# Entry of the first MLP product in a decoder layer: GpSimd's steps on VectorE, tile pairs, a norm factor read from PSUM, ten plain column tiles for six

## The chip, the cores and the metric

The kernel runs on one NeuronCore of a Trainium2 chip. TensorE (PE) multiplies into PSUM; VectorE (DVE), ScalarE (ACT) and GpSimd (POOL) do the elementwise work; SyncE (SP) and ScalarE issue transfers. Each engine runs its own queue in order and waits on semaphores. The metric is the device time of one execution in microseconds, the median of several runs.

## What is computed

One layer of a decoder trunk over 512 tokens and a width of 2048, in float32: a mixer (a recurrence and sparse attention), an MLP, and a gated addition of a per-layer embedding (PLE). Cut to the part in question:

```python
y = jnp.concatenate([rms_norm(y_lru, gnorm_lru[i]), rms_norm(y_nsa, gnorm_nsa[i])], axis=-1)
h = h + rms_norm(y @ w_out[i], norm_mix_post[i])
f = jnp.square(jax.nn.relu(rms_norm(h, norm_mlp_pre[i]) @ mlp_w1[i])) @ mlp_w2[i]
h = h + rms_norm(f, norm_mlp_post[i])
h = h + jax.nn.sigmoid(h @ ple_gate[i]) * (p[i] @ ple_proj[i])
```

`mlp_w1` is 2048 x 8192, so its product has 64 column tiles of 128.

## The kernel before

**Layout.** Activations lie transposed: 128 channels on the partitions, 512 tokens in the free dimension, so the stream of width 2048 is 16 rows of 128x512. They lie in eight tiles `y`, each a pair of rows (`y_row(k)` is one row). A float32 product is made of three matmuls (`mm3`): weights and activations are split into a high part in the TensorE format, by ScalarE, and the rest, by VectorE, and hi x hi, hi x lo and lo x hi are summed in PSUM.

**Strips.** TensorE's program is a list of strips. A strip is 128x512 of a weight matrix, four blocks of 128 (k = 0 to 3), 12 matmuls. `go` runs over the strips: at strip j it fires the hooks due at j, splits the weights of strip j + 4 (`shi` by ScalarE, `slo` by VectorE, rings of five), lets up to two finished PSUM results be evicted, and issues the matmuls of strip j, with the hooks due at its quarters in between. `at(j, fn)` hangs a function on a strip's quarter. Every engine's queue is in the order in which `go` issues; a table of constants at the top of the file says when.

**Two forms of product.** `add_plain` multiplies a few column tiles at once, four strips each, with 512 columns per matmul. Its first strips are interleaved over the tiles, so that each activation row is used by all tiles as it comes. `pair_a` takes two column tiles at once in seven half products (Winograd's form of Strassen's), 14 strips with 256 columns per matmul; it needs seven sets of activation units (`ua`), made from sums of quarters of `y` (`combo_sum`, `prep_g`, `prep_a`), and sums of weights (`sums`).

**The entry of the first MLP product** (`back`). `b0` is the first strip of five of the PLE product (`add_ple`), `bk` the first strip behind them. While those run, the mixer's norm factor is made: `rms_a` multiplies the squares' sum with ones on TensorE and takes the root on VectorE and ScalarE, `rms_b` spreads it over the partitions by eight small matmuls into a PSUM bank and copies it to `rb` (`Ro`). Then come, for each row k, `h1_a` (times `Ro`; even k on VectorE, odd k on GpSimd), `h1_b` (times the gain `norm_mix_post`, plus `x`; and ScalarE makes the high part of the unit `up[k]`, times `norm_mlp_pre`), `h1_c` (the low part; ScalarE squares the row), `h1_d` (GpSimd adds the square to `msum`), and later `h1_e` (the row times `norm_mlp_pre`). Tiles 0 to 3 and then 4 and 5 of the product are plain and are evicted once the MLP's factor `Rm` is there. From `Rm` on, `y_scale` multiplies halves of `y` by it, on VectorE and on GpSimd, and the seven sets of units are made; then 29 pairs follow.

**Transfers.** Weights come through five buffers of 512 KB (`raw`), loaded by SP, which also loads `x` and stores PLE results. The gate product at the end has the same form: plain tiles, then pairs; its norm's scaling (L1588) and two of its `combo_sum` steps are on GpSimd as well.

Of the kernel before, what the change touches and what calls it, by code (L numbers as in the profile page):

```python
# [37 lines left out]
SL = 0.7  # L38
RMT = 11.5
WO = (-12, -11, -10, -9, -7, -5)  # L40
NPL = 6
# [21 lines left out]
PMX = (14.75, 16.5, 18.5, 20.5, 22.5, 24.5, 26.5)  # L63
# [10 lines left out]
RO0 = 1.75  # L74
RO1 = 0.5
HO = 2.75
# [3 lines left out]
PMG = (13.5, 15, 18, 20)  # L80
PLE1 = 5
# [54 lines left out]
class Build:  # L136
# [138 lines left out]
    def add_col(self, src, units, evict, lead=FW, extra=()):  # L275
        q, st, extra = {}, [], list(extra)
        b, n, step = len(self.strips), src.shape[-1] // 512, 2 if extra else 1

        def load(h):
            q[h] = self.raw_tile()  # L280
            self.nc.sync.dma_start(q[h], src[:, h * 1024:(h + 1) * 1024])

        def mm(s):
            def f(j, k):
                if s + k == 0:
                    st.append(self.bank())
# [153 lines left out]
    def y_scale(self, e, a, b, i, rb):  # L440
        t = self.y[4 * a + i][:, :, b * H:(b + 1) * H]
        e.tensor_tensor(t, t, rb[:, b * H:(b + 1) * H].unsqueeze(1).to_broadcast([P, 2, H]), op=ALU.mult)  # L442

    def prep_g(self, p):
        for i in range(4):
            if p in (1, 2):
                self.y_scale(self.nc.gpsimd, p - 1, 1, i, self.T["R"])
            else:
                self.combo_sum(1 if p == 6 else 3, (self.y[i], self.y[4 + i]), None)

    def prep_a(self, ua, p, inside=False, scale=True, lo=None):
        v, g = self.nc.vector, self.nc.gpsimd
        rb = self.T["R"]
# [46 lines left out]
    def rms_b(self, name):  # L500
# [15 lines left out]
    def run(self):  # L516
# [10 lines left out]
        self.rings = {}  # L527
        dp = self.pool("dram", space=bass.MemoryType.DRAM)
# [448 lines left out]
    def mid(self):  # L977
# [66 lines left out]
        def y_out(m):  # L1044
            def f(ps):
# [4 lines left out]
                if m >= KT - 2:  # L1050
# [337 lines left out]
    def back(self):  # L1388
# [23 lines left out]
        def load_x(k):  # L1412
            t = x_tile() if k % 8 < 4 else self.z_tile("xz")
            nc.sync.dma_start(t, A["xT"][:, k:k + 2, :])
            T["xt", k], T["xt", k + 1] = t[:, 0], t[:, 1]

        def h1_a(k):
            (g if k % 2 else v).tensor_tensor(xs(k), xs(k), T["Ro"], op=ALU.mult)

        def h1_b(k):  # L1420
            y = xs(k)
            v.scalar_tensor_tensor(y, y, V[:, V_MIXPOST + k:V_MIXPOST + k + 1], T["xt", k], op0=ALU.mult, op1=ALU.add)  # L1422
            act.activation(up[k][:, 0], y, AF.Copy, scale=V[:, V_MLPPRE + k:V_MLPPRE + k + 1])
            self.store(self.h1_d[k], y)

        def h1_c(k):
            y = xs(k)
            v.scalar_tensor_tensor(up[k][:, 1], y, V[:, V_MLPPRE + k:V_MLPPRE + k + 1], f32(up[k][:, 0]),  # L1428
                                   op0=ALU.mult, op1=ALU.subtract)
            act.activation(self.msum if k == 0 else T["xt", k], y, AF.Square)  # L1430

        def h1_d(k):
            xt = T["xt", k]
            if k == KT - 1:
                sq_last.append(xt)
            elif k:
                g.tensor_tensor(self.msum, self.msum, xt, op=ALU.add)
# [3 lines left out]

        def h1_at(k):
            return b0 + max(HO, SL * (k - 3) + HO)

        def plain_a(m0):
            def f(i, ps, st):
# [3 lines left out]
                v.tensor_tensor(t, ps, T["Rm"], op=ALU.mult)  # L1450
                v.scalar_tensor_tensor(t, t, 0.0, t, op0=ALU.max, op1=ALU.mult)
# [21 lines left out]
        for k in range(0, 8, 2):  # L1473
            at(b0 - 3 if k < 4 else b0 + 2, load_x, k)
# [3 lines left out]
        if NPL > 4:  # L1478
            self.add_plain(bk + 16, [A["mlp_w1"][m] for m in range(4, NPL)], up, plain_a(4), "Rm", (-7, -6))
        for k in range(KT):  # L1480
            if k >= 8 and k % 2 == 0:
                at(h1_at(k - 7) + 3.75, load_x, k)
            at(max(h1_at(k) + GE, b0 + GE0), h1_e, k)
            for i, fn in enumerate((h1_a, h1_b, h1_c, h1_d)):
                at(h1_at(k) + i, fn, k)
        at(bk + RMT, self.sqrt_table)
        at(bk + RMT, lambda: self.rms_a([self.msum] + sq_last, D, "m"))
# [10 lines left out]
        at(bk + 28.5, open_fb)  # L1498
# [174 lines left out]
        for p, j in zip(ORDER, GX):  # L1673
            at(bg + j, self.prep_a, ue, p, True, False, g if p in GS else None)
# [97 lines left out]
```

## Time and profile before

| What | Value |
|---|---|
| Median of 3 runs | 2459.36 us (2458.16 to 2459.91) |
| Profiled execution, its own time | 2458.5 us |
| Its span, first to last instruction | 2456.7 us, 34978 instructions |
| TensorE matmuls | 2342.9 us busy, 95% of the span |
| VectorE | 1544.3 us, 63% |
| ScalarE | 1076.8 us, 44% |
| GpSimd | 243.5 us, 10% |
| Mean granted TensorE clock | 0.979 of full speed |

Matmuls are pipelined and their ends are modelled, so a busy TensorE is not TensorE at its peak: a matmul of 512 columns is shown with 0.39 us at full clock while the next starts 0.227 us after it. Steps are therefore read from one start to the next. Some matmul records are missing.

### The profile page before, as it was taken

What the parts mean: (1) busy time and instruction counts of PE and PEld (TensorE: products, weight loads), DVE (VectorE), ACT (ScalarE), POOL (GpSimd) and SP (SyncE); (2) the same over time, 40 slices, a digit from 0 to 9 for tenths busy, and PEclk for the clock granted to TensorE, in tenths of its full rate; (3) what the DMA queues carried; (4) which work ended last, traced back from release to release, by engine and by line L of the source; (5) the groups of instructions that cost most, each with busy time, mean ns of one, the idle gap of its engine ahead of it and who ended that gap; (6) DMA issues with size and microseconds to landing.
All of it is one profiled execution on the core that took longest, in us unless ns stands there. A gap on an engine that the chain in (4) does not pass through costs nothing.

```text
span 2456.7 us, 34978 instructions
## 1 busy us (share of the span) xinstructions
PE 2342.9 (95%) x13178; PEld 2046.3 (83%) x13178; DVE 1544.3 (63%) x2543; ACT 1076.8 (44%) x2008; POOL 243.5 (10%) x238
## 2 busy tenths in 40 slices
PE   7999999989999778999999998999999999997899
PEld 6788888777788658999999997888888888886688
DVE  6364755588746789888888886333333333335898
ACT  5354655478733445444444444333223223223454
POOL 4000000134400440000000000000000000112420
PEclk9999999999999889999999999999999999998999
DMA  5452232422234532343433333434333333233644
GB/s 191 159 180 93 99 108 97 133 89 84 82 129 164 191 103 98 127 138 130 136 131 134 134 135 126 159 116 133 112 112 137 121 103 131 101 112 128 223 142 138
DMA packets 114093, 316.75 MB, mean 129 GB/s; under 512 B 11298, under 2 KB 16674, under 8 KB 113924
## 3 DMA queue, kind: packets, MB, share of 16 engines
q1 hardware_dynamic: 94708, 275.13, 34.0%
q10 hardware_dynamic: 19216, 39.39, 4.2%
q8 instruction: 103, 1.69, 0.3%
q14 instruction: 66, 0.54, 0.1%
HBM read 270.37 MB, written 44.11 MB: 128 GB/s over the span
## 4 chain that ended last, share of the span: by engine, by line
PE 62%; DVE 6%; issue 2%; DMA 1%; ACT 1%; POOL 0%; ACTq 0%; DVEq 0%; SPq 0%; POOLq 0%
PE ps_mm L165 20%; PE ps_mm L163 20%; PE ps_mm L164 20%; DVE slo L156 1%; DVE cx L156 1%; DMA fk<-f_d 1%; DVE y L1592 1%; PE ps_t L487 0%; DVE y L442 0%; POOL pz L1619 0%; ACT shi L155 0%; DVE y L1422 0%; DVE cy L156 0%; DVE y L1588 0%; DMA pz<-pp_d 0%
## 5 line engine op out<-in xcount | busy, mean ns | idle before, releaser
L156 DVE TENSOR_TENSOR slo<-raw,shi 128x512 fp32r<-128x512 f32 x802 | 580.0, 729 | 743.1 <-ACT shi L155 727.4
L155 ACT ACTIVATE shi<-raw 128x512 fp32r<-128x512 f32 x804 | 502.2, 629 | 870.5 <-PE ps_mm L164 748.4
L163 PE MATMUL ps_mm<-cx,shi 128*128 128x512 f32 (+1 forms) x2044 | 707.7, 346 | 25.4 <-ACT shi L155 19.8
L164 PE MATMUL ps_mm<-cx,shi 128*128 128x512 f32 (+1 forms) x2044 | 702.1, 343 | 15.0 <-DVE cx L1428 7.5
L165 PE MATMUL ps_mm<-cx,slo 128*128 128x512 f32 (+1 forms) x2044 | 704.0, 344 | 13.0 <-DVE slo L156 10.7
L165 PE MATMUL ps_mm<-cy,slo 128*128 128x512 f32 (+1 forms) x1604 | 555.0, 346 | 6.4 <-DVE slo L156 6.4
L163 PE MATMUL ps_mm<-cy,shi 128*128 128x512 f32 (+1 forms) x1604 | 555.4, 346 | 3.7 <-ACT shi L155 2.0
L164 PE MATMUL ps_mm<-cy,shi 128*128 128x512 f32 (+1 forms) x1604 | 554.9, 346 | 4.1 <-DVE cy L1428 4.1
L163 PEld LDWEIGHTS ps_mm<-cx,shi 128*128 128x128 f32 x2044 | 393.0, 192 | 70.8 <-ACT shi L155 23.5
L165 PEld LDWEIGHTS ps_mm<-cx,slo 128*128 128x128 f32 x2044 | 392.5, 192 | 62.7 <-DVE slo L156 16.6
L164 PEld LDWEIGHTS ps_mm<-cx,shi 128*128 128x128 f32 x2044 | 393.3, 192 | 57.8 <-DVE cx L1428 8.8
L165 PEld LDWEIGHTS ps_mm<-cy,slo 128*128 128x128 f32 x1604 | 305.8, 191 | 44.6 <-DVE slo L156 8.0
L163 PEld LDWEIGHTS ps_mm<-cy,shi 128*128 128x128 f32 x1604 | 305.9, 191 | 40.8 <-ACT shi L155 2.6
L164 PEld LDWEIGHTS ps_mm<-cy,shi 128*128 128x128 f32 x1604 | 305.9, 191 | 40.5 <-DVE cy L1428 4.8
L155 ACT ACTIVATE shi<-wsum 128x512 fp32r<-128x512 f32 x204 | 126.5, 628 | 163.9 <-PE ps_mm L164 87.8
L156 DVE TENSOR_TENSOR slo<-wsum,shi 128x512 fp32r<-128x512 f32 x204 | 138.7, 687 | 44.8 <-ACT shi L155 44.8
L1530 POOL TENSOR_TENSOR msum<-msum,fsq 128x512 f32<-128x512 f32 x13 | 16.9, 1297 | 1288.7 <-ACT fsq L1526 1288.7
L1257 POOL TENSOR_SCALAR al_P<-al_P,ar_sts 128x512 f32<-128x512 f32 (+3 forms) x128 | 74.2, 601 | 63.8 <-ACT al_ph L1279 29.3
L163 PE MATMUL ps_mm<-y,shi 128*128 128x256 f32 x272 | 76.4, 281 | 1.2 <-ACT shi L155 1.2
L1247 ACT ACTIVATE al_P<-al_P,ar_stm 128x512 f32<-128x512 f32 (+3 forms) x128 | 70.4, 554 | 16.1 <-DVE ar_stm L1242 15.8
L165 PE MATMUL ps_mm<-y,slo 128*128 128x256 f32 x272 | 76.1, 280 | 0.8 <-DVE slo L156 0.8
L164 PE MATMUL ps_mm<-y,shi 128*128 128x256 f32 x272 | 75.9, 279 | 0.0
(356 smaller groups left out, 2336.3 us busy)
## 6 DMA issues: line engine op xcount, KB each, us to landing
raw<-in_mlp_w_dram SPq DMA_DIRECT2D x254, 512.0 KB, 3.7
raw<-in_w_in_dram SPq DMA_DIRECT2D x64, 512.0 KB, 3.5
raw<-in_w_out_dram SPq DMA_DIRECT2D x32, 512.0 KB, 3.5
fk<-f_d SPq DMA_DIRECT2D x32, 512.0 KB, 5.0
raw<-in_ple_gate_dram SPq DMA_DIRECT2D x32, 512.0 KB, 4.8
f_d<-z ACTq DMA_DIRECT2D x29, 512.0 KB, 2.8
y<-in_xT_dram SPq DMA_DIRECT2D x16, 256.0 KB, 6.2
raw<-in_w_v_dram SPq DMA_DIRECT2D x8, 512.0 KB, 4.3
```

Source lines behind the costliest of these rows:

```text
L155: nc.scalar.activation(hi, src, AF.Copy)
L156: (eng or nc.vector).tensor_tensor(lo, src, f32(hi), op=ALU.subtract)
L163: mm(ps, whi, ahi, start=start, stop=False)
L164: mm(ps, whi, alo, start=False, stop=False)
L165: mm(ps, wlo, ahi, start=False, stop=stop)
L1247: act.activation(PP[qt, b], PP[qt, b], AF.Exp, scale=-1.0, bias=st["mn"][:, qt, b:b + 1], accum_out=st["sm"][:, qt, b:b + 1])
L1257: pool.tensor_scalar(PP[qt, b], PP[qt, b], st["sm"][:, qt, b:b + 1], 1.0, op0=ALU.mult, op1=ALU.mult)
L1530: g.tensor_tensor(self.msum, self.msum, sq, op=ALU.add)
L1592: v.scalar_tensor_tensor(y, y, V[:, V_MLPPOST + k:V_MLPPOST + k + 1], T["h"][k], op0=ALU.mult, op1=ALU.add)
```

## The change

The scalings, sums and squares of the entry that were on GpSimd go to VectorE, and most steps take a pair of rows (1024 columns) instead of one. `norm_mix_post` is multiplied in by ScalarE when a row of the `w_out` product is evicted, so `h1_b`'s operation with a gain becomes a plain add, and the sum of squares runs in a tile of two rows, `hs`. `rms_b("o")` makes no copy: the scalings read the PSUM bank. The evicted plain tiles are squared by ScalarE. Four more column tiles are plain: four interleaved, two one by one (`add_col`), four interleaved; 27 pairs follow. One PLE strip moves to the gate product (`PLE1`). `combo_sum`'s two GpSimd cases go to VectorE in both products. The constants that place the hooks are new.

```diff
-RMT = 11.5
-WO = (-12, -11, -10, -9, -7, -5)
-NPL = 6
+HT = (1.75, 2.75, 4, 4.25, 4.75, 8.5, 10.75, 12.25)
+HB = (0, 0.5, 0.75, 1, 2)
+RMT = 12.5
+WO = (-12, -7.75, -6.75, -5.75)
+NPL = 10
...
-PMX = (14.75, 16.5, 18.5, 20.5, 22.5, 24.5, 26.5)
+PMX = (18.5, 23, 28.25, 32.25, 36.25, 40.25, 38.25)
+YS = (15.25, 0.75)
...
-RO0 = 1.75
-RO1 = 0.5
+RO0 = 0.75
+RO1 = 0.75
...
-PLE1 = 5
+PLE1 = 4
...
         if i == 1:
-            nc.gpsimd.tensor_tensor(y11, y12, y11, op=ALU.subtract)
+            nc.vector.tensor_tensor(y11, y12, y11, op=ALU.subtract)
...
-            nc.gpsimd.tensor_tensor(y12, y22, y12, op=ALU.subtract)
+            nc.vector.tensor_tensor(y12, y22, y12, op=ALU.subtract)
...
+    def y_scale(self, i):
+        t = self.y[i]
+        self.nc.vector.tensor_tensor(t, t, self.T["R"].unsqueeze(1).to_broadcast([P, 2, S]), op=ALU.mult)
...
+        if name in self.direct:
+            self.T["R"] = self.T["R" + name] = ps2
+            return
...
                 act.activation(self.msum if m == 0 else l, y, AF.Square)
-                if m >= KT - 2:
+                act.activation(y, y, AF.Copy, scale=self.vec[:, V_MIXPOST + m:V_MIXPOST + m + 1])
+                if m == KT - 1:
...
+        def h1_a(i):
+            y, x, r = self.y[i], T["xt", i], T["Ro"]
...
+                v.tensor_tensor(y, y, r.unsqueeze(1).to_broadcast([P, 2, S]), op=ALU.mult)
+                v.tensor_tensor(y, y, x, op=ALU.add)
+                h1_hi(2 * i)
+                h1_hi(2 * i + 1)
...
+        def h1_add(i):
+            if i:
+                v.tensor_tensor(T["hs"], T["hs"], T["xt", i], op=ALU.add)
...
-                v.tensor_tensor(t, ps, T["Rm"], op=ALU.mult)
-                v.scalar_tensor_tensor(t, t, 0.0, t, op0=ALU.max, op1=ALU.mult)
+                v.scalar_tensor_tensor(t, ps, 0.0, T["Rm"], op0=ALU.max, op1=ALU.mult)
+                act.activation(t, t, AF.Square)
...
+        for m in range(4, NPL - 4):
+            self.add_col(A["mlp_w1"][m], up, lambda ps, m=m: plain_a(4)(m - 4, ps, one), 8, cond="Rm")
```

How the instructions stand, at two places. VectorE at the first rows behind the mixer's factor (`rbo`, now `ps_t`), before; `y_6710` is the first pair of rows, `y_6711` the second, `cy` and `cx` are units, `slo` is the low part of a weight strip:

```order
L1418 TENSOR_TENSOR y_6710<-y_6710,rbo 128x512
L1418 TENSOR_TENSOR y_6711<-y_6711,rbo 128x512
L156 TENSOR_TENSOR slo<-raw,shi 128x512
L1418 TENSOR_TENSOR y_6712<-y_6712,rbo 128x512
L1422 SCALAR_TENSOR_TENSOR y_6710<-y_6710,vec,xt 128x512 x2
L1422 SCALAR_TENSOR_TENSOR y_6711<-y_6711,vec,xt 128x512 x2
```

VectorE at the same place, now:

```order
L1418 TENSOR_TENSOR y_6710<-y_6710,xt 128x512
L157 TENSOR_TENSOR slo<-raw,shi 128x512
L1431 SCALAR_TENSOR_TENSOR cy<-y_6710,vec,cy 128x512 x2
L1421 TENSOR_TENSOR y_6711<-y_6711,ps_t 128x1024
L1422 TENSOR_TENSOR y_6711<-y_6711,xt 128x1024
L157 TENSOR_TENSOR slo<-raw,shi 128x512
L1431 SCALAR_TENSOR_TENSOR cy<-y_6711,vec,cy 128x512 x2
```

A pair of rows is now finished, units and all, before the next pair is scaled, and a weight split stands between the pair's add and its low parts. ScalarE a little later, at the fourth and fifth pair (`y_6713`, `y_6714`), before; `shi` is the high part of a weight strip, and rows that square `y` write `xt` or `xz`:

```order
L1423 ACTIVATE cx<-y_6713,vec 128x512
L1430 ACTIVATE xz<-y_6713 128x512
L419 DMA h_d<-y_6713 128x512
L155 ACTIVATE shi<-raw 128x512
L1423 ACTIVATE cx<-y_6714,vec 128x512
L1430 ACTIVATE xz<-y_6713 128x512
```

ScalarE at the same place, now:

```order
L1428 ACTIVATE cx<-y_6713,vec 128x512 x2
L1428 ACTIVATE cx<-y_6714,vec 128x512 x2
L1437 ACTIVATE xz<-y_6712 128x1024
L420 DMA h_d<-y_6712 128x2x512
L156 ACTIVATE shi<-raw 128x512
L1437 ACTIVATE xz<-y_6713 128x1024
L420 DMA h_d<-y_6713 128x2x512
```

A weight split there now stands behind the high parts of two whole pairs and the square of a third.

## Rows read from the trace of the kernel before

**Rows 1.** Stretches: us, then busy PE, PEld, DVE, ACT, POOL, PEclk, DMA share, GB/s.

```profile
809.40:871.60 62.20, 44.62 (x168) 33.22 (x166) 49.35 (x50) 32.73 (x56) 32.20 (x22) 0.88 0.49 169
871.60:929.50 57.90, 46.21 (x174) 36.40 (x175) 49.97 (x61) 25.43 (x47) 26.55 (x16) 0.83 0.27 91
929.50:976.80 47.30, 42.76 (x338) 41.91 (x336) 43.86 (x69) 22.68 (x40) 0.00 (x0) 0.96 0.33 112
976.80:996.90 20.10, 20.10 (x170) 20.10 (x169) 17.35 (x28) 8.72 (x15) 0.00 (x0) 1.00 0.39 132
```

**Rows 2.** VectorE's waits, 809 to 872: us in total, times, longest us.

```profile
DVE slo L156 <- ACT shi L155: 9.8, 8, 1.8
```

**Rows 3.** Line 1418, the scaling by the factor: min/median/max ns, first and last start.

```profile
L1418 DVE TENSOR_TENSOR y<-y,rbo x8: 679/1230/1785, 809.4 to 858.6; 128x512 f32<-128x512 f32 x8
L1418 POOL TENSOR_TENSOR y<-y,rbo x8: 1301/1735/1796, 809.4 to 858.1; 128x512 f32<-128x512 f32 x8
```

**Rows 4.** Timeline (start, us, engine, line) of the mixer's norm, ScalarE and TensorE.

```profile
798.54 0.63 ACT L1049 ACTIVATE yl<-y 128x512 f32<-128x512 f32 x1 [3.20 <-DVE y L1048]
...
802.33 0.28 PE L487 MATMUL ps_t<-ones,msum 128*128 128x1 f32 x2
...
804.92 0.48 PE L163 MATMUL ps_mm<-cy,shi 128*128 128x512 f32 x1
...
806.66 2.04 PE L505 MATMUL ps_t<-ident,rsmo 128*128 128x128 f32 x8
...
808.74 0.60 ACT L508 ACTIVATE rbo<-ps_t 128x512 f32<-128x512 f32 x1 [1.74 <-PE ps_t L505]
```

**Rows 5.** Timeline of VectorE, two places where nothing disturbs it.

```profile
816.77 2.06 DVE L1422 SCALAR_TENSOR_TENSOR y<-y,vec,xt 128x512 f32<-128x512 f32 x3
...
2337.22 1.22 DVE L316 TENSOR_TENSOR wsum<-raw 128x1024 f32<-128x1024 f32 x1
2338.35 0.69 DVE L156 TENSOR_TENSOR slo<-raw,shi 128x512 fp32r<-128x512 f32 x1
2338.96 1.22 DVE L320 TENSOR_TENSOR wsum<-wsum,raw 128x1024 f32<-128x1024 f32 x1
```

**Rows 6.** Groups of ScalarE's instructions by line: count, busy us, mean ns, idle before.

```profile
L1423 ACT ACTIVATE cx<-y,vec 128x512 fp32r<-128x512 f32 x10 | 7.2, 724 | 18.1 <-DVE y L1422 17.9
L155 ACT ACTIVATE shi<-raw 128x512 fp32r<-128x512 f32 x11 | 6.8, 619 | 2.7 <-PE ps_mm L164 2.7
...
L1120 ACT ACTIVATE al_kh<-raw 128x1024 fp32r<-128x1024 f32 x4 | 4.2, 1044 | 0.0
```

**Rows 7.** Timeline of TensorE at the MLP's norm.

```profile
871.59 0.58 PE L487 MATMUL ps_t<-ones,msum 128*128 128x1 f32 x2 [2.14 <-POOL msum L1437]
...
875.02 0.77 PE L163 MATMUL ps_mm<-cx,shi 128*128 128x512 f32 x1
...
881.40 1.05 PE L505 MATMUL ps_t<-ident,rsmm 128*128 128x128 f32 x8
882.21 0.47 PE L163 MATMUL ps_mm<-cx,shi 128*128 128x512 f32 x1
```

**Rows 8.** Timeline: a plain strip's weight split; starts of the third and fourth pair.

```profile
1718.22 0.69 DVE L156 TENSOR_TENSOR slo<-raw,shi 128x512 fp32r<-128x512 f32 x1 [2.03 <-ACT shi L155]
...
976.80 0.29 PE L163 MATMUL ps_mm<-cx,shi 128*128 128x256 f32 x1
...
996.91 0.29 PE L163 MATMUL ps_mm<-cx,shi 128*128 128x256 f32 x1
```

**Rows 9.** Line 1047, VectorE on a PSUM source: min/median/max ns, first and last start.

```profile
L1047 DVE TENSOR_TENSOR y<-ps_mm,rbn x16: 680/683/693, 716.6 to 797.1; 128x512 f32<-128x512 f32 x16
```

**Rows 10.** The gate product: one stretch as in rows 1, and GpSimd's groups by line.

```profile
2295.00:2325.00 30.00, 25.50 (x99) 19.91 (x98) 28.59 (x22) 15.00 (x26) 25.16 (x15) 0.90 0.57 197
...
L431 POOL TENSOR_TENSOR y<-y,y 128x512 f32<-128x512 f32 x4 | 6.8, 1741 | 0.0
L427 POOL TENSOR_TENSOR y<-y 128x512 f32<-128x512 f32 x4 | 6.8, 1734 | 38.9 <-DVE cy L156 38.9
```

More of the change, by code (lines that the diff above doesn't have):

```diff
@@ L79 @@
 SF = 0.7
-PMG = (13.5, 15, 18, 20)
-PLE1 = 5
+PMG = (24.25, 24.75)
+PLE1 = 4
 BK = -0.5
@@ L273, in add_plain, with add_col @@
                 self.strips.append(Strip(lambda i=i, s=s: q[i, s // 2][:, (s % 2) * 512:(s % 2 + 1) * 512], mm(i, s)))
-    def add_col(self, src, units, evict, lead=FW, extra=()):
+    def add_col(self, src, units, evict, lead=FW, extra=(), cond="zp"):
         q, st, extra = {}, [], list(extra)
@@ L291, in f @@
                 if s == n - 1 and k == 3:
-                    self.wait.append(("zp", evict, st[0]))
+                    self.wait.append((cond, evict, st[0]))
             return f
@@ L438, in combo_split, with prep_a @@
         self.split(u[:, :, 0, :], u[:, :, 1, :], src, eng=eng)
-    def y_scale(self, e, a, b, i, rb):
-        t = self.y[4 * a + i][:, :, b * H:(b + 1) * H]
-        e.tensor_tensor(t, t, rb[:, b * H:(b + 1) * H].unsqueeze(1).to_broadcast([P, 2, H]), op=ALU.mult)
+    def y_scale(self, i):
+        t = self.y[i]
+        self.nc.vector.tensor_tensor(t, t, self.T["R"].unsqueeze(1).to_broadcast([P, 2, S]), op=ALU.mult)
     def prep_g(self, p):
         for i in range(4):
[L446 to L453, printed above, removed]
+            self.combo_sum(1 if p == 6 else 3, (self.y[i], self.y[4 + i]), None)
+    def prep_a(self, ua, p, inside=False, lo=None):
         Y = [(self.y[i], self.y[4 + i]) for i in range(4)]
-        scale = scale and p in (1, 2)
-        if scale:
-            self.y_scale(v, p - 1, 0, 0, rb)
         if p == ORDER[-1] and inside:
@@ L466, in ready @@
         def ready(i):
-            if scale and i:
-                self.y_scale(v, p - 1, 0, i, rb)
             if p == 6:
@@ L527, in run @@
         self.rings = {}
+        self.direct = ("o",)
         dp = self.pool("dram", space=bass.MemoryType.DRAM)
@@ L1414, in load_x @@
             nc.sync.dma_start(t, A["xT"][:, k:k + 2, :])
[L1415 to L1424, printed above, removed]
@@ L1426, in h1_c @@
-        def h1_c(k):
-            y = xs(k)
-            v.scalar_tensor_tensor(up[k][:, 1], y, V[:, V_MLPPRE + k:V_MLPPRE + k + 1], f32(up[k][:, 0]),
-                                   op0=ALU.mult, op1=ALU.subtract)
[L1430 to L1437, printed above, removed]
+            T["xt", k // 2] = t
@@ new lines, in h1_a @@
+        def h1_a(i):
+            y, x, r = self.y[i], T["xt", i], T["Ro"]
+            if i == 0:
+                for a in range(2):
+                    v.tensor_tensor(y[:, a], y[:, a], r, op=ALU.mult)
+                    v.tensor_tensor(y[:, a], y[:, a], x[:, a], op=ALU.add)
+                    h1_hi(a)
+            else:
+                v.tensor_tensor(y, y, r.unsqueeze(1).to_broadcast([P, 2, S]), op=ALU.mult)
+                v.tensor_tensor(y, y, x, op=ALU.add)
+                h1_hi(2 * i)
+                h1_hi(2 * i + 1)
+            self.store(self.h1_d[2 * i:2 * i + 2].rearrange("a p n -> p a n"), y)
@@ new lines, in h1_hi, with h1_lo, h1_sq @@
+        def h1_hi(k):
+            act.activation(up[k][:, 0], xs(k), AF.Copy, scale=V[:, V_MLPPRE + k:V_MLPPRE + k + 1])
+        def h1_lo(k):
+            v.scalar_tensor_tensor(up[k][:, 1], xs(k), V[:, V_MLPPRE + k:V_MLPPRE + k + 1], f32(up[k][:, 0]),
+                                   op0=ALU.mult, op1=ALU.subtract)
+        def h1_sq(i):
+            if i == 0:
+                T["hs"] = self.sum_tile("hs").rearrange("p (a n) -> p a n", a=2)
+            act.activation(T["xt", i] if i else T["hs"], self.y[i], AF.Square)
@@ L1477, in back @@
         self.add_plain(bk, [A["mlp_w1"][m] for m in range(4)], up, plain_a(0), "Rm", (-8.5, -7.5, -6.5, -5.5))
[L1478 to L1485, printed above, removed]
+        one = {}
+        for m in range(4, NPL - 4):
+            self.add_col(A["mlp_w1"][m], up, lambda ps, m=m: plain_a(4)(m - 4, ps, one), 8, cond="Rm")
+        bl = len(self.strips)
+        self.add_plain(bl, [A["mlp_w1"][m] for m in range(NPL - 4, NPL)], up, plain_a(NPL - 4), "Rm", (-8, -7, -6, -5))
+        for i in range(KT // 2):
+            j = b0 + HT[i]
+            if i >= 4:
+                at(b0 + HT[i - 4] + 2.25, load_x, 2 * i)
+            for o, fn, k in zip(HB, (h1_a, h1_lo, h1_lo, h1_sq, h1_add), (i, 2 * i, 2 * i + 1, i, i)):
+                at(j + o, fn, k)
+            for a in range(2):
+                at(j + GE, h1_e, 2 * i + a)
         at(bk + RMT, self.sqrt_table)
-        at(bk + RMT, lambda: self.rms_a([self.msum] + sq_last, D, "m"))
+        at(bk + RMT, lambda: self.rms_a([T["hs"][:, 0], T["hs"][:, 1]], D, "m"))
+        for i in range(KT // 2):
+            at(bk + YS[0] + YS[1] * i, self.y_scale, i)
         at(bk + RMT + 1.25, self.rms_b, "m")
@@ L1491, in back @@
         for m in range(NPL, DFF // P, 2):
-            self.pair_a(b, A["mlp_w1"], m, ua, sink_a(m), first=m == NPL and NPL == 4, offs=WO if m == NPL and NPL > 4 else None, last=m == DFF // P - 2)
+            self.pair_a(b, A["mlp_w1"], m, ua, sink_a(m), offs=WO if m == NPL else None, last=m == DFF // P - 2)
             b += 14
-        for p, j in zip(ORDER, PMG):
+        for p, j in zip(ORDER[2:4], PMG):
             at(bk + j, self.prep_g, p)
@@ L1497, in back @@
             at(bk + j, self.prep_a, ua, p, True)
-        at(bk + 28.5, open_fb)
+        at(bl + 20.5, open_fb)
         base = len(self.strips)
```

8 lines of the change are left out of this document (2 added, 6 removed).

## Prediction, made before the changed kernel had run

> **What bounds the kernel now.** TensorE is busy for 2342.9 of 2456.7 us, so only stretches in which it waits, or runs at its lower clock, can give time back. I read the busy times stretch by stretch first, then who waits for whom, then the instructions of a line. The stretch that the change rewrites runs from the first scaling by the mixer's norm factor (809.4) to the end of the first ten column tiles of the product with `mlp_w1` (976.8, where the third pair starts). TensorE is busy for 44.62 of the first 62.20 us, 46.21 of the next 57.90 and 42.76 of 47.30, at granted clocks of 0.88, 0.83 and 0.96; from 976.8 on it is busy throughout at 1.00 [rows 1]. VectorE is the fullest engine beside it, 49.35 us of the 62.20 [rows 1], and it still waits eight times, 9.8 us in all, for ScalarE's splits of the weights [rows 2]. Much of its time is no work of its own: the same scaling of 128x512 takes it 0.679 us alone and up to 1.785 us while GpSimd, at a median of 1.735 us, does the other half of it [rows 3]. So the bound is a chain through VectorE and ScalarE, made longer by GpSimd, and TensorE waits at the end of it.
>
> Three marks give the time: R, when the norm factor of the mixer can be used; Q, when the sum of squares for the MLP's norm is complete and TensorE may multiply it; E, when ten column tiles are done. Before, R is 809.4, Q 871.6, E 976.8. All steady work behind E is the same in both programs, so what E gains is gained.
>
> **Term A, the factor earlier.** Before, the product of the squares stands behind 1.75 strips of the PLE product and begins at 802.33; the last square is ready at 798.54 + 0.63 = 799.2 [rows 4]. After, it stands behind 0.75 strips, and TensorE is there by then. It has two accumulators, not three: 16 matmuls for 24, (804.92 - 802.33) x 16/24 = 1.7 us. Then 0.75 strips: the half strip took 806.66 - 804.92 = 1.74 us, so 2.6. Then the transposes, 2.04 us. That is 805.5, and VectorE reads the bank directly; the copy of 0.60 us that began at 808.74 is gone [rows 4]. **A = 805.5 - 809.4 = -3.9 us**; at full clock (2.72 x 0.75 [rows 8] and 1.05 [rows 7] for the last two) -5.4, with ScalarE's new gain copy in the way -2. That copy, one in each tile of the second half of `w_out`, costs nothing elsewhere: a tile there takes (797.1 - 716.6)/15 = 5.4 us [rows 9], and ScalarE is idle for 3.20 us ahead of the square [rows 4]. One PLE strip fewer stands ahead of the entry and one more ahead of the gate product; at both places TensorE waits for a norm chain anyway, so I cost it at nothing, 2.7 us if one cover is gone.
>
> **Term B, R to Q.** VectorE's steps, start to start, are 0.60 us for 512 columns and 1.13 for 1024 [rows 5], and (2.06 - 0.74)/2 = 0.66 with a gain [rows 5]. ScalarE's rows are 0.72 with a gain (the split and the late gain alike), 0.62 for a weight split, 1.04 for 1024 columns [rows 6]. All of VectorE's queue between R and Q is now 21 x 1.13 + 18 x 0.60 + 16 x 0.66 = 45.1 us: GpSimd's eight scalings and fourteen sums of squares are in it, and nothing is stretched. But it can't run through: the order puts the split of the next weight strip behind the two gained splits of a tile pair on ScalarE, and on VectorE that strip's low part ahead of work that is ready. Followed through both queues in that order, always taking what comes last, the path from R to Q has 20 x 1.13 + 14 x 0.60 + 9 x 0.66 = 36.9 us on VectorE and, alternating with it, 19 x 0.72 + 10 x 0.62 + 4 x 1.04 = 24.1 us on ScalarE: 61.0, and 61.5 with the hand-overs. **B = 61.5 - 62.2 = -0.7 us.** What GpSimd's absence saves, its work on VectorE takes again. Ends: 45.1 us if ScalarE never is late (-17); 45.1 + 36 (all of ScalarE's queue there) = 81 if nothing overlaps (+19). The path has 16 us of waits where rows 2 have 9.8, nearer to it than to none or to 36, so I keep it. The gain of the mixer's norm leaves VectorE here (L1422 becomes a plain add), which is in these counts.
>
> The scalings read the factor from PSUM. VectorE's operation with a PSUM source takes 683 ns [rows 9], one without 0.69 us [rows 5], so I give it no price. [...]
>
> **Term C, Q to E.** Before: 976.8 - 871.6 = 105.2 us, for 12.5 plain strips and two pairs. After: the product of the squares at the lower clock, 875.02 - 871.59 = 3.4 us [rows 7]; 27.5 plain strips, since Q now stands at strip 12.5 of 40, at 0.69 + 2.03 = 2.72 us (one weight split and the idle time ahead of it, in a steady stretch [rows 8]) = 74.8; the transposes, 882.21 - 881.40 = 0.8 [rows 7]; and the lower clock behind the wait: from 875.02 to 881.40 fifteen matmuls went by [rows 7], 6.4 us where the full-clock step of 2.72/12 = 0.227 would take 3.4, so 3.0 lost. Sum 82.0. **C = -23.2 us**. This holds if nothing waits in it. VectorE has to do there 10 evictions x 0.66, 8 scalings x 1.13, 44 sums and splits of 512 columns x 0.60, 3 weight sums x 1.13 and 26 weight splits x 0.60 = 61 us in 82; the longest block between two weight splits is the twelve steps of `t2`, 8 us, under the four strips (10.9 us) of lead. So TensorE is next to be late, not VectorE. In C is the price of the two pairs made plain: a pair takes 996.91 - 976.80 = 20.11 us [rows 8], two plain tiles 8 x 2.72 = 21.76, so 2 x 1.65 = 3.3 us.
>
> **Term D, the gate product.** `combo_sum` moves eight sums to VectorE there too. In 2295 to 2325 VectorE is busy for 28.59 of 30 us and TensorE for 25.50 at clock 0.90 [rows 10], so 4.5 + 3.0 us are lost. The sums cost VectorE 8 x 0.60 = 4.8 us; gone are GpSimd's 6.8 + 6.8 us [rows 10], which stretched about eight of its steps by 1.1 = 8.8. GpSimd's output work moves up into the gap and goes on stretching. Net -4; I take the later strip order as neutral. **D = -4 us**, between -8 (all the loss back) and +5 (the sums open).
>
> **Sum.** -3.9 - 0.7 - 23.2 - 4 = -31.8 us on the profiled execution's 2458.5: 2426.7. It lies 0.9 under the median of the runs, 2459.4, so **2428 us**.
>
> **The rivals.** (1) *VectorE never waits for ScalarE*: B is 45.1, 16 us less: 2412. For it: half of ScalarE's time there is free. Against: rows 2, and the order just followed. (2) *Pairs make the hand-overs coarser*: B is 81, 20 us more: 2448. For it: a tile's split waits for two 1.13 us steps of its pair, not for one of 0.60. Against: in the latter half several sums are ready whenever a split is late. (3) *The other side*: the column tiles behind Q stay bound by VectorE, as the stretch to 929.5 is, 49.97 of 57.90 [rows 1], and each short wait drops TensorE's clock: matmul steps of 6.38/15 = 0.43 us [rows 7] for 0.227, 2.4 us a strip. The gain of 31.8 is spent at 13 of the 27.5 strips; at 16 it is 2466, at all of them 2494. For it: the clock of 0.83 there [rows 1]. Against: 61 us of work in 82. (4) *The tiles don't hide anything*: weights come late, since SP's queue holds loads of `x` and PLE stores among them, so C keeps its 105 us: with A, B and D that is near 2451; with the gate at its bad end 2460, no change.
>
> **How the numbers follow.** Forecast 0.50, (1) 0.18, (2) 0.16, (3) 0.08, (4) 0.08. The range of 2411 to 2448 holds the forecast and most of (1) and (2), and leaves out (3), (4) and the far halves of two tails, near 0.2. The measurement tells 0.2% (4.9 us) from no change. Faster: forecast, (1), (2) and half of (4), 0.88; same: the rest of (4), with a little of (3), 0.05; slower: 0.07.
>
> **What would show it.** R near 805.5 and VectorE steps without stretch; Q near 867, with TensorE idle some 5 us ahead of it and ScalarE ending VectorE's waits; then 27 strips at 2.72 us; the first pair of tiles starting near 949, with no wait inside. Q near 851 means rival 1, near 886 rival 2; strips of 5 us behind Q rival 3; a wait for the weights' transfers rival 4. Most likely wrong is B, since it hangs on the order of two queues, and D.

## The result, and the profile of the changed kernel

The changed kernel takes 2427.4 us in the median (four runs, 2425.6 to 2429.4); the kernel before takes 2459.6 beside it. The ratio is 0.987, with a 95% interval of 0.985 to 0.989. The profiled execution has a span of 2427.6 us for 2456.7, 29.1 less.

The same stretches as in [rows 1], with the marks of the changed kernel: the product of the mixer's squares to R, R to Q, Q to the start of the first pair, and the first pair. Columns: us, then busy PE, PEld, DVE, ACT, POOL, PEclk, DMA share, GB/s.

```profile
800.90:805.50 4.60, 4.50 (x32) 3.90 (x31) 2.32 (x9) 2.61 (x7) 0.00 (x0) 1.00 0.54 157
805.50:866.50 61.00, 45.17 (x180) 34.53 (x179) 46.72 (x55) 36.16 (x57) 0.00 (x0) 0.91 0.57 199
866.50:947.20 80.70, 80.67 (x354) 67.41 (x355) 58.42 (x90) 36.13 (x66) 0.00 (x0) 0.96 0.33 115
947.20:969.70 22.50, 20.85 (x171) 20.40 (x171) 20.48 (x34) 12.87 (x24) 0.00 (x0) 1.00 0.37 130
```

Up to Q TensorE still waits for a quarter of the time (45.17 busy of 61.00). Behind Q the picture has changed: where [rows 1] have 46.21 busy of 57.90 and 42.76 of 47.30, it is now busy for 80.67 of 80.70 us, and VectorE has over 22 us to spare.

The timeline that answers to [rows 4] (start, us, engine, line):

```profile
799.81 0.63 ACT L1044 ACTIVATE yl<-y 128x512 f32<-128x512 f32 x1 [2.49 <-DVE y L1043]
...
800.89 0.28 PE L478 MATMUL ps_t<-ones,msum 128*128 128x1 f32 x2
...
802.59 0.48 PE L164 MATMUL ps_mm<-cy,shi 128*128 128x512 f32 x1
...
803.82 0.40 PE L166 MATMUL ps_mm<-cy,slo 128*128 128x512 f32 x1
804.32 1.13 PE L496 MATMUL ps_t<-ident,rsmo 128*128 128x128 f32 x8
```

The last square is ready at 800.44 and the product of the squares begins at 800.89, behind strips that TensorE runs without a gap: it is 0.45 us late, where before it was 3.2 (799.2 and 802.33, [rows 4]). Six matmuls of the PLE product and the transposes follow, and R is 805.48. Then come the waits of VectorE between R and Q, beside [rows 2], and TensorE's at the end (waiter, releaser: us, times, longest):

```profile
DVE slo L157 <- ACT shi L156: 13.1, 10, 2.2
...
PE ps_t L478 <- DVE hs L1441: 7.7, 1, 7.7
```

The waits for ScalarE have grown from 9.8 to 13.1 us while GpSimd's work has gone. The steps themselves, beside [rows 3] (min/median/max ns, first and last start):

```profile
L1417 DVE TENSOR_TENSOR y<-y,ps_t x2: 681/684/686, 805.5 to 806.8; 128x512 f32<-128x512 f32 x2
...
L1421 DVE TENSOR_TENSOR y<-y,ps_t x7: 1210/1212/1216, 811.5 to 857.5; 128x1024 f32<-128x1024 f32 x7
...
L1422 DVE TENSOR_TENSOR y<-y,xz x4: 1224/1226/1227, 819.0 to 858.7; 128x1024 f32<-128x1024 f32 x4
```

No step is stretched. The scaling, whose factor lies in PSUM, takes no longer (1212 ns) than the sum from SBUF alone (1226). TensorE at the MLP's norm, beside [rows 7], and the start of the first pair, beside [rows 8]:

```profile
866.53 3.55 PE L478 MATMUL ps_t<-ones,hs 128*128 128x1 f32 x16 [7.67 <-DVE hs L1441]
869.93 0.77 PE L164 MATMUL ps_mm<-cx,shi 128*128 128x512 f32 x1
...
874.92 1.05 PE L496 MATMUL ps_t<-ident,rsmm 128*128 128x128 f32 x8
875.73 0.48 PE L164 MATMUL ps_mm<-cx,shi 128*128 128x512 f32 x1
...
947.25 0.28 PE L164 MATMUL ps_mm<-cx,shi 128*128 128x256 f32 x1
```

Last the gate product, from the product of the last norm's squares to the products with the seventh unit of its first pair (`ps_mm<-y`): before, and then in the changed kernel.

```profile
2239.80:2367.10 127.30, 101.97 (x478) 83.82 (x477) 105.52 (x124) 53.24 (x95) 57.13 (x30) 0.88 0.47 164
```

```profile
2212.30:2337.60 125.30, 106.38 (x490) 88.11 (x489) 97.15 (x133) 54.62 (x98) 46.42 (x22) 0.86 0.48 172
```

VectorE does nine instructions more and is busy for 8.4 us less. The stretch is 2.0 us shorter although TensorE has 12 matmuls more in it (490 for 478): the PLE strip that the change moved here. Its idle time falls from 25.3 to 18.9 us. Two of its waits in the changed kernel, of which the second doesn't occur before (engine, releaser: us, times, longest):

```profile
PE ps_mm L165 <- DVE cx L1605: 7.2, 1, 7.2
...
PE ps_mm L164 <- ACT ppo L1376: 2.7, 1, 2.7
```

The first is for the low part of a unit at the entry of the gate product, the second for ScalarE's eviction of a PLE result.

Where the 29.1 us between the two traces came from, mark by mark (minus is gained):

| stretch | before | after | difference |
|---|---|---|---|
| start to the product of the norm ahead of the mixer's output product | 688.73 | 690.01 | +1.3 |
| from there to R | 120.64 | 115.48 | -5.2 |
| R to Q | 62.2 | 61.0 | -1.2 |
| Q to ten column tiles | 105.2 | 80.7 | -24.5 |
| the pair behind them | 20.1 | 22.3 | +2.2 |
| from its end to the last norm's product | 1242.9 | 1242.8 | -0.1 |
| last norm's product to the end | 216.9 | 215.3 | -1.6 |

The first row is the same code in both kernels. Of the second row's 5.2 us, 2.7 are the PLE strip that stood ahead of the product of the squares and now runs in the last row's stretch.

### The profile page after: what moved, and what is told of

It is laid out like the page before. It is cut to its first block, busy times and chain, and to the rows that moved or that the text cites. A ratio compares the mean times of both kernels' runs of the same rounds, so it can differ in the third digit from the quotient of the medians.

```text
span 2427.6 us, 34521 instructions
## 1 busy us (share of the span) xinstructions
PE 2338.8 (96%) x13026; PEld 2039.1 (84%) x13026; DVE 1502.3 (62%) x2523; ACT 1083.3 (45%) x2011; POOL 173.6 (7%) x192
## 4 chain that ended last, share of the span: by engine, by line
PE 70%; DVE 5%; ACT 3%; issue 2%; DMA 1%; POOL 0%; ACTq 0%; SPq 0%; DVEq 0%; POOLq 0%
PE ps_mm L164 22%; PE ps_mm L166 22%; PE ps_mm L165 22%; PE ps_o L1290 1%; DMA fk<-f_d 1%; PE ps_t L1263 1%; ACT shi L156 1%; DVE slo L157 1%; ACT al_P L1243 1%; PE ps_s L1230 0%; PE ps_t L478 0%; PE ps_s L1231 0%; DVE al_q L1112 0%; POOL pz L1627 0%; DVE y L1600 0%
## 5 line engine op out<-in xcount | busy, mean ns | idle before, releaser
L157 DVE TENSOR_TENSOR slo<-raw,shi 128x512 fp32r<-128x512 f32 x806 | 566.0, 708 | 755.3 <-ACT shi L156 739.0
L166 PE MATMUL ps_mm<-cy,slo 128*128 128x512 f32 (+1 forms) x1584 | 549.4, 347 | 0.9 <-DVE slo L157 0.9
L164 PEld LDWEIGHTS ps_mm<-cy,shi 128*128 128x128 f32 x1584 | 300.8, 190 | 42.7 <-ACT shi L156 3.2
L166 PEld LDWEIGHTS ps_mm<-cy,slo 128*128 128x128 f32 x1584 | 300.3, 190 | 38.8 <-DVE slo L157 1.6
L165 PEld LDWEIGHTS ps_mm<-cy,shi 128*128 128x128 f32 x1584 | 300.4, 190 | 37.5 <-DVE cy L1431 1.1
L156 ACT ACTIVATE shi<-wsum 128x512 fp32r<-128x512 f32 x192 | 119.0, 628 | 147.6 <-PE ps_mm L165 83.7
L157 DVE TENSOR_TENSOR slo<-wsum,shi 128x512 fp32r<-128x512 f32 x192 | 130.4, 686 | 41.9 <-ACT shi L156 41.8
L164 PE MATMUL ps_mm<-y,shi 128*128 128x256 f32 x256 | 72.1, 282 | 0.4 <-ACT shi L156 0.4
L165 PE MATMUL ps_mm<-y,shi 128*128 128x256 f32 x256 | 71.4, 279 | 0.0
```

Of the source, the lines that this page charges most:

```text
L156: nc.scalar.activation(hi, src, AF.Copy)
L157: (eng or nc.vector).tensor_tensor(lo, src, f32(hi), op=ALU.subtract)
L164: mm(ps, whi, ahi, start=start, stop=False)
L165: mm(ps, whi, alo, start=False, stop=False)
L166: mm(ps, wlo, ahi, start=False, stop=stop)
```

## The experiments

Each kernel is the changed one (once: the one before) with one edit, and at the end with two and three. Most ran once. Effects of a few us are read as distances between marks in the trace. In every trace with the changed kernel's order ahead of R, the product of the earlier norm to R is 115.48 us, to the hundredth, but for the kernel that copies the factor.

### GpSimd's sums in the gate product

```diff
+        e = nc.gpsimd if self.pool_sums else nc.vector
...
-            nc.vector.tensor_tensor(y11, y12, y11, op=ALU.subtract)
+            e.tensor_tensor(y11, y12, y11, op=ALU.subtract)
...
-            nc.vector.tensor_tensor(y12, y22, y12, op=ALU.subtract)
+            e.tensor_tensor(y12, y22, y12, op=ALU.subtract)
...
+        self.pool_sums = False
...
+        at(last, setattr, self, "pool_sums", True)
```

> The changed kernel, with the eight sums of combo_sum (kinds 1 and 3) on GpSimd again in the gate product, and nowhere else. Measured by the stretch from the product of the squares of the last norm to the end of the trace, 215.3 us in the changed kernel, 216.9 before. Theory D of the prediction (GpSimd's sums held VectorE and cost 4 us): 219 us. Rival (the sums' place is not on the path there, what was gained comes from the order of strips): 215.3, within 0.7.

From the last norm's product to the end: 217.85 us, between the two figures. The stretch of the gate, as above:

```profile
2212.30:2340.90 128.60, 105.95 (x489) 85.76 (x488) 106.10 (x125) 54.90 (x98) 56.82 (x30) 0.88 0.48 167
```

VectorE is back at 106.10 us, as before the change (105.52), and 2.55 us are lost. Kernels with the same gate scatter here: 215.1 to 215.7 in seven traces, 214.3 and 214.7 in two and 212.7 in another; with the sums on GpSimd 216.9, 217.85 and 218.8. The two groups don't overlap, so theory D holds in its direction: GpSimd's sums held VectorE, and moving them gains time. The size, 2.55 for 4, is known only within this scatter. It is more than the 1.6 us of the table: the moved PLE strip and the new order, which both kernels compared here have, would then have cost some 1 us, which is less than the scatter.

### GpSimd's work in the entry, in the changed kernel and in the one before

```diff
-        self.direct = ("o",)
+        self.direct = ()
...
-                    v.tensor_tensor(y[:, a], y[:, a], r, op=ALU.mult)
+                    (g if a else v).tensor_tensor(y[:, a], y[:, a], r, op=ALU.mult)
...
-                v.tensor_tensor(y, y, r.unsqueeze(1).to_broadcast([P, 2, S]), op=ALU.mult)
+                v.tensor_tensor(y[:, 0], y[:, 0], r, op=ALU.mult)
+                g.tensor_tensor(y[:, 1], y[:, 1], r, op=ALU.mult)
...
-                v.tensor_tensor(T["hs"], T["hs"], T["xt", i], op=ALU.add)
+                g.tensor_tensor(T["hs"], T["hs"], T["xt", i], op=ALU.add)
```

> The changed kernel with GpSimd's work of the entry given back: one half of each scaling by the mixer's factor and all seven sums of squares, as 128x1024, run on GpSimd; the factor is copied to SBUF by ScalarE for that. Measured from the first scaling (R) to the product of the sums of squares (Q), 61.05 us in the changed kernel. Theory B (what GpSimd's absence saves, its work on VectorE takes again, the path is set by hand-overs with ScalarE): 61 to 64 us. Rival (VectorE's steps, stretched beside GpSimd, set the stretch): each of seven sums of some 3.4 us stretches VectorE by half of that, 12 us, and each shared scaling costs 1.75 for 1.13, 5 us: 73 to 78 us.

R to Q took 67.6 us, 6.6 more: between the two, so neither number held. The groups between R and Q show the mechanism of the rival (count, busy us, mean ns, idle before):

```profile
L157 DVE TENSOR_TENSOR slo<-raw,shi 128x512 fp32r<-128x512 f32 x13 | 15.2, 1182 | 12.7 <-ACT shi L156 12.7
...
L1422 POOL TENSOR_TENSOR y<-y,rbo 128x512 f32<-128x512 f32 x7 | 12.1, 1745 | 0.0
...
L1442 POOL TENSOR_TENSOR hs<-hs,xz 128x1024 f32<-128x1024 f32 x4 | 10.0, 2510 | 21.2 <-ACT xz L1438 21.1
```

The weight splits take 690 ns each in the changed kernel. The mean of 1182 here mixes two kinds: eight splits during which GpSimd is idle take 678 to 695 ns, and the five that run beside one of its steps 1475 to 2516. The longest of them, and the sums beside it (start, us):

```profile
835.87 5.17 POOL L1442 TENSOR_TENSOR hs<-hs,xz 128x1024 f32<-128x1024 f32 x2 [9.75 <-ACT xz L1438]
836.28 2.52 DVE L157 TENSOR_TENSOR slo<-raw,shi 128x512 fp32r<-128x512 f32 x1 [2.21 <-ACT shi L156]
```

VectorE's waits for ScalarE stay (12.7 us for 13.1), and the stretching comes on top of them. The copy of the factor shows too: from the product of the squares to R 5.23 us for 4.59.

The other way round, the kernel before with this one part of the change:

```diff
-            (g if k % 2 else v).tensor_tensor(xs(k), xs(k), T["Ro"], op=ALU.mult)
+            v.tensor_tensor(xs(k), xs(k), T["Ro"], op=ALU.mult)
...
-                g.tensor_tensor(self.msum, self.msum, xt, op=ALU.add)
+                v.tensor_tensor(self.msum, self.msum, xt, op=ALU.add)
```

> The kernel before with one part of the change alone: the eight scalings and fifteen sums of squares that GpSimd did in the entry run on VectorE, as steps of 128x512 in the same order; nothing else moves. Measured from R (first scaling) to Q (product of the sums of squares), 62.2 us before. Theory B as predicted (what GpSimd's absence saves, its work on VectorE takes again): 62, within 1.5. Rival, from the run that gave the work back to GpSimd in the changed kernel and lost 6.6 us by it: 55 to 57 us, and then it is the order and the pairs of the changed kernel that took the gain again.

R to Q took 58.4 us for 62.2, again between the two. The move from GpSimd to VectorE is worth 3.9 us of this stretch in the old order; the time of the whole kernel, 2455.8 us in one run, can't be told from the kernel before beside it (2453.6 to 2462.6). The changed kernel's own stretch, 61.0, is 2.7 longer than this. "Takes again" was wrong: something else of the change takes it.

### What holds R to Q at 61 us

Two edits of the changed kernel, each for one suspect. First the late gains, which ScalarE does ahead of weight splits that VectorE waits for:

```diff
-GE = 8
+GE = 13
```

> The changed kernel with the sixteen late gains of ScalarE (h1_e) five strips later, so that they stand behind the weight splits up to the sum of squares. Theory B (VectorE waits for the weight split on ScalarE, with the gains ahead of it): following both queues gives R to Q 3.5 us shorter, 57.5 for 61.05, and the whole kernel as much, near 2424. Rival (VectorE's own work sets it): R to Q stays at 61.0, within 0.5.

R to Q took 57.8 us, 3.2 less. VectorE's waits there:

```profile
DVE slo L157 <- ACT shi L156: 10.0, 7, 2.2
```

They fall by the same 3.1 us (13.1 to 10.0), and VectorE's busy time stays (46.56 us for 46.72). So the path does alternate between the two engines, as term B followed it. The whole kernel did not get faster by as much: 2426.8 us in its one run, within the range of the changed kernel's (2425.6 to 2429.4) and not near 2424. In the trace 1.2 of the 3.2 us are given back between Q and the second pair.

Then the pairs:

```diff
-            if i == 0:
+            if True:
                 for a in range(2):
                     v.tensor_tensor(y[:, a], y[:, a], r, op=ALU.mult)
                     v.tensor_tensor(y[:, a], y[:, a], x[:, a], op=ALU.add)
-                    h1_hi(a)
+                    h1_hi(2 * i + a)
```

> The changed kernel with the scaling and the residual sum of each pair cut again into two steps of 128x512, the high part of a half following its own sum; all of it on VectorE. Theory from the cost of a step (two of 0.60 us for one of 1.13): 14 pairs of steps, R to Q 1.0 us longer, 62.0. Rival (the hand-over to ScalarE is made coarser by pairs, so that its high part starts later): following both queues gives 2 us less, 59.

R to Q took 59.2 us, 1.9 less. The stretch, first of the changed kernel with halves, columns as above:

```profile
803.00:862.10 59.10, 45.38 (x180) 34.91 (x178) 48.16 (x69) 36.93 (x57) 0.00 (x0) 0.90 0.60 206
```

VectorE is busy for 1.44 us more (48.16 for 46.72), 14 merged steps being undone, and the stretch is shorter all the same. ScalarE now begins the high part of a half when that half is done, and the weight split behind it comes earlier: VectorE waits 10.3 us for it and not 13.1. Merging saved VectorE's time, which was not short, and cost the hand-over, which was. This is the second rival of the prediction, as a part of the stretch: undoing it gives 1.9 us, where the changed kernel is 2.7 behind the old order. The whole kernel took 2426.4 us in one run, again within the changed kernel's range, and 0.9 us are given back between Q and the second pair.

### How many plain column tiles the cover needs

```diff
-NPL = 10
+NPL = 8
```

> The changed kernel with eight plain column tiles (4, 4), the rest as it is. Measured from Q to the start of the pair that makes columns 10 and 11, 83.1 us with ten. Theory C (cover): 61 us of VectorE's work of the 83, less eight weight splits and two evictions (6 us), stand against 61 us of strips; TensorE just about waits: 82 to 90 us, and the idle time of TensorE behind Q rises from 1.7 us to 2 to 8. Rival (there is cover to spare): 81.5 us, one pair cheaper by 1.65, idle time as with ten.

The mark needs a word: a pair that waits takes longer than the steady 20.1 us, so "the start" is put 20.1 us ahead of the end of the pair that makes columns 10 and 11. In the changed kernel that is 82.9 us behind Q, though the pair's first matmul starts at 80.7 (the expectations read the mark some 0.2 us later). So read, it took 93.5 us for 82.9, more than either expected, and the kernel took 2436.3 us, some 9 more than the changed one. Its first pair starts at 925.9; the stretch ahead of it, the first pair, and the waits that name its cause (866 to 960):

```profile
906.10:926.00 19.90, 19.90 (x90) 16.47 (x89) 17.91 (x29) 5.59 (x9) 0.00 (x0) 1.00 0.31 105
926.00:959.40 33.40, 26.01 (x171) 24.59 (x170) 30.11 (x49) 19.93 (x38) 0.00 (x0) 0.85 0.27 95
```

```profile
PE ps_mm L164 <- ACT shi L156: 3.3, 3, 2.4
...
PE ps_mm L165 <- DVE cx L157: 3.1, 1, 3.1
```

The plain strips run through; the pair takes 33.3 us and not 20.1, while VectorE is busy for 30.1 of it with the units and the sums that two more tiles would have covered. About 7.4 us of the 13.2 lost are waiting, and the rest the lower clock (0.85 over the pair) that comes with it. My estimate counted the wait and left out the clock.

With six tiles in a group of four and one of two:

```diff
-NPL = 10
+NPL = 6
-PMX = (18.5, 23, 28.25, 32.25, 36.25, 40.25, 38.25)
+PMX = (14.75, 16.5, 18.5, 20.5, 22.5, 24.5, 26.5)
-YS = (15.25, 0.75)
+YS = (13.5, 0.25)
-PMG = (24.25, 24.75)
+PMG = (14.25, 14.5)
...
```

> The changed kernel with six plain column tiles (4, 2) again, not ten; scalings, sums and splits of the pairs' units at the places that they had before, still all on VectorE. Measured from Q to the start of the pair that makes columns 10 and 11 (83.1 us in the changed kernel; 79.8 if two pairs, 3.3 us cheaper, hid all the same), against 105.2 before. Theory C (the plain tiles are the cover of VectorE's work): VectorE has the same units to make, in 43.5 us of TensorE's work less ahead of the first pair, so TensorE waits again: 90 to 105 us. Rival (GpSimd's stretching was the cause of the waits behind Q, six tiles cover the rest): 80 to 83 us, and the kernel is 0 to 3 us faster than the changed one.

It took 96.1 us, at 2441.5 in all. Two of the eight scalings stood ahead of the MLP's factor there and took the mixer's; a second kernel has them behind it (`YS = (14, 0.1)`):

> The kernel of plain6 with all eight scalings behind the MLP's factor (two of them stood ahead of it there and took the mixer's factor, 0.25 strips early). Measured from Q to the start of the pair that makes columns 10 and 11, 96.3 us in plain6, 83.1 with ten plain tiles. Theory C (cover): as in plain6, 95 to 98 us. Rival (plain6 was slow for its two early scalings): 90 or less.

It took 100.3 us, 2447.5 in all, somewhat over what theory C gave. In both, the late gains of the last pairs of rows stand behind sums that use those rows, so the units hold other values than the reference's; the operations are the same in kind and number. The stretch from 33.6 us behind Q to the end of the first pair, of the second of them:

```profile
900.00:946.90 46.90, 39.52 (x222) 34.16 (x220) 42.38 (x67) 28.03 (x52) 0.00 (x0) 0.85 0.20 68
```

VectorE is busy for 42.38 of 46.90 us, with no GpSimd at all, and TensorE waits at a clock of 0.85. The rival (GpSimd alone was the cause of the waits behind Q) is out: with GpSimd's work moved, and six tiles, 96 to 100 of the former 105 us remain. Ten tiles bring it to 82.9. Ten tiles with GpSimd's work left where it was were not run, so how much the tiles would gain without the move isn't shown.

### A version that is faster than both

Both edits that shortened R to Q, in one kernel:

> The changed kernel with both edits that shortened R to Q: the late gains five strips later, and the scaling and residual sums in halves. If their gains add up (61.0 - 3.2 - 1.9): R to Q 55.9 us, and the kernel 5 us faster than the changed one, near 2422 us, 0.985 of before. Rival (they take away the same wait): R to Q 57.5, near 2424.

R to Q took 56.2 us, 4.9 less, so in this stretch the gains add up but for 0.2. Its time was 2424.9 us, nearer to the rival's figure than to 2422, and 0.987 of the kernel before with an interval of 0.985 to 0.989; since the runs of before spread over 9 us beside it, it was timed again, with the changed kernel at its side:

> The changed kernel as it is, beside the next two on one chip, so that their times can be set against it. Every theory: 0.987 of before, as in its first runs.

> The kernel with both edits (late gains later, scaling and sums in halves) once more. Its trace has R to Q 4.9 us shorter than the changed kernel's; if nothing gives that back, it is 0.998 of the changed kernel here. Rival (given back behind Q): the two agree within 0.1%.

The changed kernel took 2426.8 us (2425.5 to 2429.3), the kernel with both edits 2423.4 (2419.6 to 2425.0): 0.9986, 3.4 us less, and their runs are apart by 0.5 us. Against before they are 0.988 (0.986 to 0.989) and 0.986 (0.984 to 0.987). In the trace R to Q is 56.2 us once more, and the stretches behind Q agree with the changed kernel's within 1 us.

The runs of the entry suggested the same step at the gate, where GpSimd still does half of the scalings:

```diff
-            (g if k % 2 else v).tensor_tensor(y, y, T["Rf"], op=ALU.mult)
+            v.tensor_tensor(y, y, T["Rf"], op=ALU.mult)
```

> The kernel with both edits, and the eight scalings that GpSimd does at the entry of the gate product on VectorE. What was seen at the first entry (3.9 us in the order of before, 6.6 us with the sums in pairs) carries over: the stretch from the last norm's product to the end 2 to 4 us shorter, 211 to 212.5 us for 214.3, the kernel near 2421. Rival (VectorE has no room there: 8 x 0.60 us more of its own): 214 to 217.

It took 2419.9 us (2418.0 to 2420.9), 0.984 of before (0.983 to 0.986): the fastest kernel here, 7 us under the changed one. From the last norm's product to the end it is 209.9 us for 214.7, more than expected. The gate's stretch, first with both edits alone, then with the scalings moved as well:

```profile
2208.60:2333.40 124.80, 103.62 (x490) 85.40 (x489) 98.02 (x134) 54.65 (x98) 44.29 (x22) 0.89 0.49 175
```

```profile
2208.40:2328.20 119.80, 103.47 (x489) 83.97 (x488) 93.97 (x141) 54.42 (x98) 32.71 (x14) 0.93 0.51 179
```

VectorE does eight scalings more (seven of them in the records) and is busy for 4 us less. TensorE's wait for the low part of a unit at the entry, 7.2 us with both edits alone as in the changed kernel, is shorter:

```profile
PE ps_mm L165 <- DVE cx L1605: 2.0, 1, 2.0
```

The traces of the older gate lie between 212.7 and 215.7 us, so the direction is clear and the size is not known to the microsecond.

## Why the prediction held, point by point

**Term A** gave -3.9 us with an end at -5.4; measured, from a mark that both kernels pass in the same way, -5.2. The order of events was right: 16 matmuls, a piece of the PLE product, transposes, no copy. "TensorE is there by then" holds but for 0.45 us. Two sizes in it were wrong. The piece is six matmuls, half a strip, and not the 0.75 strips that I read off the constant: 802.59 to 804.32, 1.7 us for 2.6. And the transposes, which I took from [rows 4], ran there at a lower clock; a stretch of the kernel before shows it, where the changed kernel's own row above has 1.00:

```profile
802.30:809.40 7.10, 7.10 (x42) 6.20 (x41) 1.64 (x8) 2.30 (x5) 0.00 (x0) 0.77 0.89 288
```

They take 1.13 us, not 2.04. That R stands at 805.5 in the trace, as predicted to the tenth, is chance: the profiled execution was 1.3 us late on reaching this place. The copy, 0.6 in the prediction, is 0.64 in the run that has it.

**Term B** gave 61.5 us for R to Q; measured 61.0. The method held. Following both queues gave a path that alternates between VectorE and ScalarE with 16 us of waits on VectorE; the trace has 13.1 us of them, and the runs moved as the same method said: 3.5 us for the late gains (3.2 measured) and 2 for the halves (1.9). TensorE's wait ahead of Q, "some 5 us", is 7.67. The sentence beside it failed, that GpSimd's absence saves no more than its work on VectorE takes again. It is worth 3.9 us in the order of before and 6.6 us in the new one. The changed kernel ends up only 1.2 us ahead because its order gives 2.7 us back, of which undoing the pairs returns 1.9; the other 0.8 us was not separated. So B's sum came out near for the order that was followed, and the reason given beside it was wrong.

**The factor in PSUM** was given no price, and 1212 ns against 1226 bears it out. So does the same scaling of 128x512 in two other kernels: a median of 681 ns with the factor in PSUM (the kernel with halves), 685 with it in SBUF (the kernel before with its scalings on VectorE).

**Term C** gave 82.0 us from Q to the first pair; measured 80.7. Strips at 2.72 us with nothing waiting among them were right. The 3.0 us for the lower clock behind the wait were 1.6: the fifteen matmuls between the product and the transposes took 874.92 - 869.93 = 5.0 us for 3.4 at full clock, not 6.4. What failed is "with no wait inside" for the pair that follows. TensorE waits there twice, for ScalarE's and VectorE's split of the same weight strip. On ScalarE that split (`shi`) stands behind four high parts of a unit:

```profile
952.96 0.61 ACT L156 ACTIVATE cx<-y 128x512 fp32r<-128x512 f32 x1
...
953.48 1.66 ACT L156 ACTIVATE cx<-y 128x512 fp32r<-128x512 f32 x3
...
955.04 0.61 ACT L156 ACTIVATE shi<-wsum 128x512 fp32r<-128x512 f32 x1
...
955.71 0.39 PE L164 MATMUL ps_mm<-cy,shi 128*128 128x256 f32 x1 [1.11 <-ACT shi L156]
...
956.76 0.39 PE L166 MATMUL ps_mm<-cy,slo 128*128 128x256 f32 x1 [0.54 <-DVE slo L157]
```

The pair takes 22.3 us for 20.1. So term C, -23.2 as predicted, is -24.5 + 2.2 = -22.3. I summed VectorE's 61 us against the 82 up to the first pair (58.4 of 80.7, measured) and did not look at the pair, where it is busy for 20.48 of 22.50 and where the order on ScalarE matters again. The runs with eight and six tiles show how near the edge this is: two tiles fewer already cost 10.6 us there.

**Term D** gave -4 us; measured -1.6 between the two traces, and 2.55 by moving the sums back. The relief of VectorE was right, even too small: 8.4 us less busy, where 8.8 of stretching gone and 4.8 of sums added make 4. But I priced it by VectorE's time, as if it were all on TensorE's path. Between the two kernels that differ by the sums alone, VectorE is busy for 9.0 us less and TensorE's stretch is 3.3 us shorter (128.6 to 125.3). The PLE strip was costed at nothing, or 2.7 us if a cover is gone. Its 12 matmuls do fill a wait: TensorE waits 0.59 us for the first unit of the gate product where it waited 5.59. But the 2.7 us for the eviction of a PLE result are new. With the sums moved back, strip and new order are 1.0 us slower than before (217.85 for 216.87), which is less than the scatter there. What was left to gain is mostly the wait for a unit's low part, 7.2 us, of which the last run takes 5.2 by moving GpSimd's scalings.

**The sum** was -31.8 us. Less the 1.3 us at the start of the profile, the traces have 29.1 + 1.3 = 30.4, near to it. The medians of the runs, 2459.6 and 2427.4, differ by 32.2. Terms A and C came out within 1.3 us and D 2.4 short; the errors partly cancel.

**The rivals.** That VectorE never waits for ScalarE (1) is out: ten waits, 13.1 us. Coarser hand-overs (2) are real, at 1.9 us and not 20. Tiles behind Q bound by VectorE (3) is not the changed kernel, 80.67 us busy of 80.70; with eight tiles its first pair is, and there the lower clock makes up near half of the 13.2 us lost. No wait for a weight's transfer (4) shows behind Q.

## What to carry to other kernels

When an engine shares work with one that slows it down, count what the sharing costs in stretched steps on all that runs beside it, and not only on the work that moves; in this kernel moving a share to the faster engine (a scaling of 128x512 took VectorE 684 ns and GpSimd 1745) shortened its stretch of the trace at each of the three places where it was tried, by 3.9, 3.3 and 5.0 us, though that engine was the fullest beside TensorE. Where two engines hand work to each other, follow both queues in order: here merged steps saved VectorE 1.44 us and made the stretch 1.9 us longer, work without a deadline ahead of a hand-over made it 3.2 us longer, and taking both away gave 4.9 of 61 us. Work that is to hide a preparation must last up to the last use of what is prepared, the first steps behind it included. The price of falling short can be more than the wait: with eight tiles 7.4 us of waits came with a clock of 0.85 over the pair, while in the changed kernel the pair's two waits, 1.65 us, left it at 1.00.

## What the runs showed of the hardware that was not expected

- A VectorE split of 128x512, 678 to 695 ns alone, took 1475 to 2516 ns beside a step of GpSimd (eight and five splits, in the changed kernel with GpSimd's work in the entry given back). In the gate, moving eight scalings to VectorE made its busy time fall from 98.02 to 93.97 us.
- Between 802.3 and 809.4 us of the kernel before, TensorE ran at a mean granted clock of 0.77 though it was busy throughout (7.10 of 7.10 us); the changed kernel, with 16 one-column matmuls there and not 24, kept 1.00 from the product of the squares to R. Whether the eight matmuls make the difference was not tried.
- The start of the program varies: the product of the norm ahead of the mixer's output product comes between 685.9 and 690.7 us in the traces of these kernels, whose code up to there is the same. A gain of 2 us can't be read from one time, but it can from the distance between two marks: R to Q was 61.03 to 61.05 us in each of six traces with that stretch unchanged.
